# Residual rows turned by VectorE and by loads in runs of 128 bytes instead of TensorE, and filling products dealt 2-4

## The chip, the core and the metric

One core of a Trainium2 chip. The metric is the device time of one execution in microseconds (us); of a kernel several runs are timed and their median is given. TensorE (PE in the profile) multiplies matrices, and also turns tiles by a product with the identity; VectorE (DVE), ScalarE (ACT) and GpSimd (POOL) work elementwise; SyncE (SP) issues almost all DMA transfers, in order, to one queue. DRAM, SBUF (128 partitions) and PSUM (where products land) are the memories.

## What is computed

A trunk of two layers over 1024 tokens of width 1024 in float32: a retention layer, then one projection to keys and values that the second layer shares, then a layer of stick-breaking attention with 8 heads. Both layers end in the same way; the last lines are the ones that matter here.

```python
def reference(x, ..., sb_norm_pre, sb_w_in, sb_w_out, sb_norm_post):
    ...
            u = rms_norm(h, sb_norm_pre[j])
            proj = u @ sb_w_in[j]
            q, g = jnp.split(proj, [SB_QK_WIDTH], axis=-1)
            q = split_heads(q, SB_HEADS).astype(jnp.float32)
            o = stick_breaking_attention(q, k_shared, v_shared)
            o = merge_heads(o).astype(h.dtype) * jax.nn.silu(g)
            y = o @ sb_w_out[j]
            h = h + rms_norm(y, sb_norm_post[j])
    return h
```

`h` on the right of the last line is the residual.

## The kernel before

**Layout.** Tokens are worked in two halves, t=0 (tokens 0 to 511) and t=1 (512 to 1023). In nearly all of the kernel a tile has channels on the partitions and tokens along the row, the turned form; the residual is kept in DRAM in that form, as `h_d[t][u]`, four tensors of 128x1024 per half, each holding two blocks of 128 channels by 512 tokens side by side. A float32 product is made as three products of a high and a low part (`mm3`, lines 413, 414 and 415). `split` (lines 514, 515) makes the two parts: ACT the high one, VectorE the low one.

**The second layer.** Sixteen attention heads-and-halves `n` = 0 to 15 (two heads to an `Att` object, eight objects). For each, `rows` makes scores, VectorE scans them, and `mix` turns the weights on PE (line 1298), multiplies them with the values and calls `gate`, which loads the gate (`sg<-g`), multiplies it with the product in PSUM (line 1326) and splits the result into `oT`. `merge(main, side, ...)` writes one list of steps with others dealt evenly in between. While the first heads run, PE is also fed with the last projection products of the layer before (`P.pieces`, the filler): they end in VectorE's sums of line 888 (`tab<-pma`, `S<-pmb`).

**The end.** The last object's output product is made by `finish(1, heads[7], ys)`. Its steps `prep(0..3)` are dealt into n = 15: they load the output weights (`whl`, `ko`, `A`), the residual (`xh<-h`, one tile of 128x1024 per `u`, four loads of 512 KB in rows of 4 KB) and the gain row (`sgn`). Then `last()` makes, for each of four blocks b of 128 tokens, the output with tokens on the partitions: `piece` (12 products into one bank for 512 channels; VectorE adds what earlier objects gave, ACT sums squares, VectorE scales the sum and multiplies with the gain), `turn(b)` (eight products with the identity that turn the residual of the block from channels to tokens on the partitions, into two PSUM banks, line 1398), and `write(b)` (POOL takes the power −1/2 into `col`, line 1403; VectorE multiplies the row with it and adds the turned residual, line 1406; two stores to the output). The last block's second half is made as two pieces of 256.

**What sets the order.** The program is first written as one list of instructions; then `arrange`, a planner with costs for each operation and due times, sets the order of each engine's queue. So an edit in one place can move rows elsewhere. Tiles come from rings by tag (`xh` 8, `vo` 4, `sg` 4, `AT` 3 buffers and so on), and a tile waits until the readers of the one before it in the ring are done.

Of the kernel before, what the change touches and what calls it, by code (L numbers as in the profile page):

```python
# [13 lines left out]
F32 = mybir.dt.float32  # L14
F32R = mybir.dt.float32r
AF = mybir.ActivationFunctionType
ALU = mybir.AluOpType
# [291 lines left out]
def trunk(ctx, tc, xT, wts, gains, trig, ident_in, cols, last_gain, out):  # L309
# [5 lines left out]
    nc = tc.nc  # L315
# [7 lines left out]
    def S(tag, shape, dt=F32):  # L323
        cnt[0] += 1
        x = sb.tile([128] + list(shape), dt, tag=tag, name=f"{tag}{cnt[0]}", bufs=BUFS[tag])
        tag_of[x[:].tensor.name] = tag
        return x

    def PS(tag):
        cnt[0] += 1  # L330
        x = ps.tile([128, 512], F32, tag=tag, name=f"p{tag}{cnt[0]}", bufs=BUFS[tag])
        tag_of[x[:].tensor.name] = tag
        banks.add(x[:].tensor.name)
        return x
# [24 lines left out]
    def dma(dst, src, eng=nc.sync):  # L359
        return eng.dma_start(dst.bitcast(F32), src.bitcast(F32))  # L360

    keep = tc.keep_in_program_order
    V, A_, G, MM = nc.vector, nc.scalar, nc.gpsimd, nc.tensor.matmul
# [99 lines left out]
    def merge(main, *sides):  # L463


        done = [0] * len(sides)
        for i, m in enumerate(main):
            m()
            for k, (steps, lead, tail) in enumerate(sides):
                n = len(main) - lead - tail  # L470
                upto = min(len(steps), len(steps) * max(0, i + 1 - lead) // n)
                while done[k] < upto:
                    steps[done[k]]()
                    done[k] += 1
# [48 lines left out]

    turned = out[0:512, :].rearrange("a (b t) -> (a b) t", b=2)
    straight = out[512:1024, :]
    st_d = [[dr.tile([128, 512], F32, tag=f"st{h}{d}", name=f"st{h}{d}") for d in range(2)] for h in range(NH)]
    y_d = [[dr.tile([128, 512], F32, tag=f"y{t}{c}", name=f"y{t}{c}") for c in range(8)] for t in range(2)]
    h_d = [[DRAM(f"h{t}{c}", F32) for c in range(4)] for t in range(2)]
# [803 lines left out]
    def c_post(t, y_d, acc):  # L1332
# [22 lines left out]

        return [stat1, stat2, row] + in_turn(8, 1, load, add)

    def finish(t, P, ys):

        w, hs, box = {}, [], {}  # L1360

        def prep(u):
            nh, i = divmod(u, 2)
            x = S("whl", [2, 2, 512], F32R) if u == 0 else None
            for e in range(2):
                r = w[nh, 2 * i + e] = x[:, :, e] if u == 0 else hl("ko" if u == 1 else "A")
                for k in range(2):
                    dma(r[:, :, 256 * k:256 * k + 256],
                        w_d[P.pr][2 * nh + k][i][:].rearrange("p (l e n) -> p l e n", l=2, e=2)[:, :, e])
            a = S("xh", [1024])  # L1370
            dma(a[:], h_d[t][u][:])
            hs.append(a)
            if u == 3:
                box["g"] = S("sgn", [1024])
                dma(box["g"][:], last_gain.broadcast_to([128, D]))

        def piece(b, k, a, n):
            if a == 0:
                box["s"], box["y"] = S("small", [4]), S("AT", [1024])
            p, tl = PS(banks4[box.setdefault("n", 0) % 4]), slice(128 * b, 128 * b + 128)  # L1380
            box["n"] += 1
            nh, cl = a // 512, slice(a % 512, a % 512 + n)
            for e in range(4):
                x, o = w[nh, e], P.oT[e]
                mm3(p[:, :n], o[:, 0, tl], o[:, 1, tl], x[:, 0, cl], x[:, 1, cl], e == 0, e == 3)
            y, q, sm = ys[b][:, nh, cl], S("f2", [512]), box["s"]
            V.tensor_tensor(y, p[:, :n], y, ALU.add)
            A_.activation(q[:, :n], y, AF.Square, accum_out=sm[:, k:k + 1])
            if k == 0:
                V.tensor_scalar(sm[:, 3:4], sm[:, 0:1], 1.0 / D, EPS, ALU.mult, ALU.add)  # L1390
            else:
                V.tensor_scalar(sm[:, 3:4], sm[:, k:k + 1], 1.0 / D, sm[:, 3:4], ALU.mult, ALU.add)
            V.tensor_tensor(box["y"][:, a:a + n], y, box["g"][:, a:a + n], ALU.mult)

        def turn(b):
            box["h", b] = [PS("o" if b % 2 else "z") for _ in range(2)]
            for c in range(8):
                nc.tensor.transpose(box["h", b][c // 4][:, 128 * (c % 4):128 * (c % 4) + 128],
                                    hs[c // 2][:, 512 * (c % 2) + 128 * b:512 * (c % 2) + 128 * b + 128], ident[:])

        def write(b):
            r, y = S("col", [4]), box["y"]
            G.tensor_tensor(r[:, 0:1], box["s"][:, 3:4], mhalf[:, 0:1], ALU.pow)
            for nh in range(2):
                cl = slice(512 * nh, 512 * nh + 512)
                V.scalar_tensor_tensor(y[:, cl], y[:, cl], r[:, 0:1], box["h", b][nh][:], ALU.mult, ALU.add)
                dma(straight[128 * b:128 * b + 128, cl], y[:, cl], nc.scalar if nh else nc.sync)

        def last():
            for b in range(4):  # L1410
                piece(b, 0, 0, 512)
                if b < 3:
                    turn(b)
                for k, a in ((1, 512),) if b < 3 else ((1, 512), (2, 768)):
                    piece(b, k, a, 512 if b < 3 else 256)
                if b == 3:
                    turn(b)
                write(b)

        return [lambda u=u: prep(u) for u in range(4)], last  # L1420
# [131 lines left out]
    def layer_c(units, out, load, kept, post):  # L1552

        kq, gs, vs, _ = units
        order = [(x, n) for x in kq[:3] + [vs[0]] for n in (1, 2)]
        opening = len(order)
        order += [(x, n) for x in [vs[0]] + kq[:3] for n in rest]
        order += [(x, n) for x in kq[3:] + [vs[1]] + gs[:2] for n in full]
        order += [(x, n) for x in gs[2:] for n in (1, 5, 6, 7, 4)]
        fill = len(order)  # L1560
        order += [(x, n) for n in (2, 3) for x in gs[2:]]
        P = Phase(order, (opening, fill))
        first, end, halt = P.marks
        at = P.at
        merge(out[:14], (load, 0, 2))
        P.ensure(1)
        merge(out[14:])

        def scale(kt):
            V.tensor_tensor(kept[kt][:], kept[kt][:], rowh[0][:].unsqueeze(1).broadcast_to([128, 2, 512]), ALU.mult)  # L1570
        post += c_stats(1)
        for j, k in zip((1,2,3,3,4,5,6,7,8,9,10,12,13,14), range(len(post))):
            at[j].append(post[k])
        for j, f in zip((first - 4,first - 3,first - 2,first - 1), w_turn(B.raws, kept, scale)):
            at[j].append(f)
        trays[:] = ["sc0", "sc1", "A"]
        at[first].append(lambda: trays.__setitem__(slice(None), ["sc0", "sc1", "A", "A", "A", "A"]))
        at[first].append(lambda: ring.__setitem__(slice(None), ["wraw", "wraw", "wraw", "vo", "vo"]))
        pres = w_out()
        for k, f in enumerate(pres):  # L1580
            at[first + 30 + (end - first - 30 - 28) * k // len(pres)].append(f)
        heads = [Att(t, p) for t in range(2) for p in range(NPAIR)]

        def rows_of(n):
            return heads[n // 2].rows(n % 2) if n < 16 else []
        r0 = []
        for k in range(4):
            at[end - 4 + k].append(lambda k=k: (r0 or r0.extend(rows_of(0)), r0[k]()))
        for f in P.pieces(0, end):
            f()  # L1590
        filler = P.pieces(end, halt)
        merge(heads[0].mix(0), (filler[:3], 0, 1))
        merge(rows_of(1), (filler[3:6], 0, 0))
        merge(heads[0].mix(1), (filler[6:], 0, 1), (rows_of(2), 0, 1))
        ys, acc = [], []
        for n in range(2, 16):
            A = heads[n // 2]
            if n % 2 == 0:
                L = heads[n // 2 - 1]
                if n % 8 == 2:  # L1600
                    ys = []
                pre, out = L.out(ys, acc if L.t == 0 and L.pr == 3 else None)
                pre[0]()
            extra = []
            if n == 9:
                post = c_post(0, y_d[1], acc)
            if 10 <= n < 14:
                extra = post[3 * n - 30:3 * n - 27]
            if n == 15:
                extra, last = finish(1, heads[7], ys)  # L1610
            merge(A.mix(n % 2), (out[8 * (n % 2):][:8], 0 if n % 2 else 1, 1), (rows_of(n + 1), 0, 1), (extra, 1, 1))
        last()
# [79 lines left out]
```

## Time and profile before

| | us |
|---|---|
| median of 3 runs | 1629.36 |
| the runs | 1628.98 to 1630.21 |
| the profiled execution, its own time | 1628.69 |
| its span (first to last instruction) | 1626.7 |
| PE busy in it | 1619.3 |
| VectorE busy in it | 1219.1 |
| ACT, POOL busy in it | 804.1, 122.1 |

The profile describes the one profiled execution. Its own time is 2.0 us longer than its span, for what lies ahead of the first and behind the last instruction. The median of the timed runs is 0.67 us above the profiled execution. The DMA queues move 386.43 MB in 175890 packets. TensorE's granted clock is full throughout. In rows of the profile, names are the program's tile names without their numbers: `pma`, `pmb`, `pz` and `po` are PSUM banks.

### The profile page before, as it was taken

Reading aid. Unit: us, or ns where it says so; the run is one execution under the profiler, and the core shown is the slowest. Engines: PE = TensorE matmul, PEld = TensorE weight load, DVE = VectorE, ACT = ScalarE, POOL = GpSimd, SP = SyncE. Lnnn points to the kernel's source line nnn. Section 1 sums busy time; section 2 is a strip of 40 time slices with the busy share of each in tenths; the row PEclk is TensorE's granted clock in tenths of the full one; section 3 lists DMA queues with packets and bytes.
Section 4 is the critical chain, followed back from the end, with each engine's and each line's share of the span. In section 5 each row is a group of like instructions: output and inputs, shape, how many; then the busy total and the mean of one; then the engine's idle time right before and its main releaser. Section 6 shows DMA issues by size and latency. Waiting matters only on the chain.

```text
span 1626.7 us, 22505 instructions
## 1 busy us (share of the span) xinstructions
PE 1619.3 (100%) x7659; PEld 1351.5 (83%) x7659; DVE 1219.1 (75%) x1956; ACT 804.1 (49%) x1535; POOL 122.1 (8%) x271
## 2 busy tenths in 40 slices
PE   9999999999999999999999999999999999999998
PEld 7888888888888888888888888888888888888887
DVE  8997866654668888887689877767658666878775
ACT  8553334433456555544356665566544433554432
POOL 0000000000022212211000000000001111010010
PEclk9999999999999999999999999999999999999999
DMA  9556765543377878784776788978337877869781
GB/s 319 188 175 252 247 211 189 208 141 133 112 267 254 308 246 285 234 290 146 242 278 223 260 312 290 344 278 308 119 126 259 314 279 259 282 214 331 253 272 52
DMA packets 175890, 386.43 MB, mean 238 GB/s; under 512 B 18080, under 2 KB 34592, under 8 KB 173216
## 3 DMA queue, kind: packets, MB, share of 16 engines
q1 hardware_dynamic: 175056, 383.93, 68.3%
q8 instruction: 60, 0.98, 0.2%
q10 hardware_dynamic: 720, 1.07, 0.2%
q14 instruction: 54, 0.44, 0.1%
HBM read 263.82 MB, written 121.11 MB: 237 GB/s over the span
## 4 chain that ended last, share of the span: by engine, by line
PE 98%; DMA 1%; DVE 0%; issue 0%; ACT 0%; SPq 0%; DVEq 0%; POOLq 0%; POOL 0%
PE pma L413 12%; PE pma L415 12%; PE pma L414 12%; PE pmb L413 9%; PE pmb L415 9%; PE pmb L414 9%; PE po L414 6%; PE po L415 6%; PE po L413 6%; PE pz L414 3%; PE pz L415 3%; PE pz L413 3%; PE pz L1298 2%; PE pz L770 1%; PE pz L488 0%; DMA wraw<-in_wts_dram 0%
## 5 line engine op out<-in xcount | busy, mean ns | idle before, releaser
L514 ACT ACTIVATE whl<-wraw 128x512 fp32r<-128x512 f32 x266 | 156.2, 625 | 175.1 <-issue 62.6
L515 DVE TENSOR_TENSOR whl<-wraw,whl 128x512 fp32r<-128x512 f32 x266 | 176.1, 686 | 87.0 <-ACT whl L514 84.4
L1270 DVE TENSOR_TENSOR_SCAN sgn<-sgn 128x128 f32<-128x128 f32 (+3 forms) x64 | 86.6, 1352 | 17.3 <-POOL sgn L1268 17.3
L515 DVE TENSOR_TENSOR AT<-pz,AT 128x512 fp32r<-128x512 f32 (+1 forms) x96 | 51.1, 551 | 50.0 <-ACT AT L514 49.6
L514 ACT ACTIVATE AT<-pz 128x512 fp32r<-128x512 f32 (+1 forms) x96 | 45.1, 492 | 68.4 <-PE pz L1298 67.9
L413 PE MATMUL pmb<-oT,whl 128*128 128x512 f32 x192 | 75.9, 395 | 0.0
L415 PE MATMUL pmb<-oT,whl 128*128 128x512 f32 x192 | 75.3, 392 | 0.0
L414 PE MATMUL pmb<-oT,whl 128*128 128x512 f32 x192 | 75.1, 391 | 0.0
L413 PE MATMUL pmb<-qk,whl 128*128 128x512 f32 x184 | 72.5, 394 | 0.0
L415 PE MATMUL pmb<-qk,whl 128*128 128x512 f32 x184 | 72.1, 392 | 0.0
L414 PE MATMUL pmb<-qk,whl 128*128 128x512 f32 x184 | 71.8, 390 | 0.0
L515 DVE TENSOR_TENSOR whl<-vo,whl 128x512 fp32r<-128x512 f32 x62 | 41.7, 689 | 35.1 <-ACT whl L514 34.8
L884 ACT ACTIVATE f<-pma 128x512 f32<-128x512 f32 x52 | 30.7, 595 | 49.7 <-PE pma L415 49.3
L514 ACT ACTIVATE whl<-vo 128x512 fp32r<-128x512 f32 x62 | 37.5, 624 | 34.7 <-PE pma L415 17.5
L413 PE MATMUL pma<-xh,whl 128*128 128x512 f32 x136 | 53.3, 392 | 0.0
L414 PE MATMUL pma<-xh,whl 128*128 128x512 f32 x136 | 53.1, 390 | 0.0
L415 PE MATMUL pma<-xh,whl 128*128 128x512 f32 x136 | 53.1, 390 | 0.0
L1267 POOL TENSOR_SCALAR_AFFINE_SELECT A<-A 128x128 f32<-128x128 f32 x32 | 10.8, 336 | 535.1 <-DMA ko<-k 395.4
L907 ACT ACTIVATE wraw<-wraw,gn 128x256 f32<-128x256 f32 x102 | 45.4, 497 | 7.9 <-DMA wraw<-in_wts_dram 7.9
L1262 ACT ACTIVATE xh<-pz 128x512 f32<-128x512 f32 (+3 forms) x48 | 23.6, 492 | 48.6 <-PE pz L415 48.4
L1263 ACT ACTIVATE sgn<-pz 128x512 f32<-128x512 f32 (+2 forms) x96 | 46.7, 488 | 0.0
L1262 ACT ACTIVATE A<-pz 128x512 f32<-128x512 f32 (+3 forms) x48 | 23.6, 491 | 42.5 <-PE pz L415 42.4
(580 smaller groups left out, 5137.0 us busy)
## 6 DMA issues: line engine op xcount, KB each, us to landing
wraw<-in_wts_dram SPq DMA_DIRECT2D x332, 256.0 KB, 3.8
whl<-w SPq DMA_DIRECT2D x56, 512.0 KB, 6.0
vo<-in_wts_dram SPq DMA_DIRECT2D x70, 256.0 KB, 4.4
xh<-k SPq DMA_DIRECT2D x32, 512.0 KB, 6.8
v<-v SPq DMA_DIRECT2D x32, 512.0 KB, 5.0
k<-A SPq DMA_DIRECT2D x21, 512.0 KB, 4.9
e<-whl SPq DMA_DIRECT2D x10, 1024.0 KB, 6.7
whl<-e SPq DMA_DIRECT2D x10, 1024.0 KB, 6.7
```

Source lines behind the costliest of these rows:

```text
L413: MM(p, lh, rh, start=start, stop=False, **kw)
L414: MM(p, lh, rl, start=False, stop=False, **kw)
L415: MM(p, ll, rh, start=False, stop=stop, **kw)
L514: A_.activation(dst[0], src, AF.Copy)
L515: V.tensor_tensor(dst[1], src, f32(dst[0]), ALU.subtract)
L770: nc.tensor.transpose(pt[:, 128 * e:128 * e + 128], on[:, 128 * e:128 * e + 128], ident[:])
L884: A_.activation(c[:], p[:], AF.Copy)
L907: A_.activation(x, x, AF.Copy, scale=gcol(self.gains[col], 2 * (2 * i + k) + c))
L1262: A_.activation(a[:, o:o + ww], p[:, :ww], AF.Sigmoid)
L1263: A_.activation(n[:, o:o + ww], p[:, :ww], AF.Sigmoid, scale=-1.0)
L1270: V.tensor_tensor_scan(n[:, :W][:, ::-1], n[:, :W][:, ::-1], n[:, :W][:, ::-1], 1.0, ALU.mult, ALU.bypass)
L1298: nc.tensor.transpose(p[:, 128 * tb:128 * tb + 128], self.A[hh][tb][:, c0:c0 + 128], ident[:])
```

## The change

The eight blocks of 128 channels of the second half's residual are turned beforehand, without PE. `turn_h(k)` loads block k, has VectorE transpose it in squares of 32x32 (each square stays where it is), and stores it to a new DRAM tensor `ht_d`. Two of these steps are dealt into each of n = 2 to 5. `prep(u)` then loads the residual of block u with tokens on the partitions: four loads, each taking 32 tokens of 32x32 pieces, 1024 runs of 32 floats (128 bytes). `turn(b)` is gone, and `write(b)` adds `hs[b]` from SBUF. Separately, the six filler steps of the first two merges are dealt two and four instead of three and three.

```diff
+    ht_d = dr.tile([1024, 512], F32, tag="ht", name="ht")
...
+    def turn_h(k):
+        a, x = S("vo", [512]), S("vo", [512])
+        dma(a[:], h_d[1][k // 2][:, 512 * (k % 2):512 * (k % 2) + 512])
+        V.transpose(x[:], a[:])
+        dma(ht_d[128 * k:128 * k + 128, :], x[:])
+
     def finish(t, P, ys):
...
             a = S("xh", [1024])
-            dma(a[:], h_d[t][u][:])
+            for j in range(4):
+                dma(a[32 * j:32 * j + 32, :].rearrange("a (k b) -> a k b", b=32),
+                    ht_d[:].rearrange("(k a) t -> a k t", a=32)[:, :, 128 * u + 32 * j:128 * u + 32 * j + 32])
             hs.append(a)
...
-        def turn(b):
-            box["h", b] = [PS("o" if b % 2 else "z") for _ in range(2)]
-            for c in range(8):
-                nc.tensor.transpose(box["h", b][c // 4][:, 128 * (c % 4):128 * (c % 4) + 128],
-                                    hs[c // 2][:, 512 * (c % 2) + 128 * b:512 * (c % 2) + 128 * b + 128], ident[:])
-
...
-                V.scalar_tensor_tensor(y[:, cl], y[:, cl], r[:, 0:1], box["h", b][nh][:], ALU.mult, ALU.add)
+                V.scalar_tensor_tensor(y[:, cl], y[:, cl], r[:, 0:1], hs[b][:, cl], ALU.mult, ALU.add)
...
-                if b < 3:
-                    turn(b)
...
-                if b == 3:
-                    turn(b)
                 write(b)
...
-        merge(heads[0].mix(0), (filler[:3], 0, 1))
-        merge(rows_of(1), (filler[3:6], 0, 0))
+        merge(heads[0].mix(0), (filler[:2], 0, 1))
+        merge(rows_of(1), (filler[2:6], 0, 0))
...
-            extra = []
+            extra = [lambda k=k: turn_h(k) for k in (2 * n - 4, 2 * n - 3)] if 2 <= n < 6 else []
```

The rows below are lines of the order of one engine's instructions, with the tiles' running numbers, first the kernel before, then the changed one. Line numbers of the changed kernel are higher: 888 becomes 889, 1013 becomes 1014, 1326 becomes 1327, 1387 becomes 1396, 1392 becomes 1401, 1393 becomes 1402, 1406 becomes 1409.

PE among the last products, before (block 0; `pma` is the bank of the products, `pz` the bank of the turned residual, `xh` the residual's tiles):

```order
L413 MATMUL pma2606_15391<-ko2589_15293,qk2560_15160 128x512
L414 MATMUL pma2606_15391<-ko2589_15293,qk2560_15160 128x512
L415 MATMUL pma2606_15391<-ko2589_15293,qk2560_15160 128x512
L1398 MATMUL pz2608_15409<-ident_70,xh2582_15254 128x128 x2
L1398 MATMUL pz2608_15409<-ident_70,xh2590_15296 128x128 x2
L1398 MATMUL pz2609_15410<-ident_70,xh2597_15341 128x128 x2
L1398 MATMUL pz2609_15410<-ident_70,xh2600_15375 128x128 x2
L413 MATMUL pma2610_15419<-A2595_15335,qk2560_15160 128x512
L414 MATMUL pma2610_15419<-A2595_15335,qk2560_15160 128x512
```

The same place in the changed kernel:

```order
L413 MATMUL pma2622_15444<-ko2605_15337,qk2576_15201 128x512
L414 MATMUL pma2622_15444<-ko2605_15337,qk2576_15201 128x512
L415 MATMUL pma2622_15444<-ko2605_15337,qk2576_15201 128x512
L413 MATMUL pma2624_15462<-A2611_15382,qk2576_15201 128x512
L414 MATMUL pma2624_15462<-A2611_15382,qk2576_15201 128x512
L415 MATMUL pma2624_15462<-A2611_15382,qk2576_15201 128x512
```

The products of the second piece follow those of the first at once; the same goes for blocks 1 and 2, and behind the last product nothing is left on PE.

SP while the last head runs, before: weights to `ko` and `whl`, the residual to four `xh` tiles, the gain, and the first store to the output.

```order
L360 DMA ko2589_15293<-w301_229 128x2x256
L360 DMA ko2589_15293<-w311_231 128x2x256
L360 DMA xh2582_15254<-h10_104 128x1024
L360 DMA xh2590_15296<-h11_105 128x1024
L360 DMA whl2581_15249<-w300_228 128x2x256
L360 DMA whl2581_15249<-w310_230 128x2x256
L360 DMA whl2581_15249<-w300_228 128x2x256
L360 DMA whl2581_15249<-w310_230 128x2x256
L360 DMA xh2597_15341<-h12_106 128x1024
L360 DMA xh2600_15375<-h13_107 128x1024
L360 DMA sgn2601_15377<-in_last_gain_dram 128x1024
L360 DMA out_0_dram<-AT2605_15390 128x512
```

The same in the changed kernel, where the four blocks' tiles are `xh2598`, `xh2606`, `xh2613` and `xh2616`:

```order
L360 DMA xh2598_15295<-ht_76 32x32x32
L360 DMA xh2606_15340<-ht_76 32x32x32
L360 DMA whl2597_15290<-w300_229 128x2x256
L360 DMA whl2597_15290<-w310_231 128x2x256
L360 DMA whl2597_15290<-w300_229 128x2x256
L360 DMA whl2597_15290<-w310_231 128x2x256
L360 DMA xh2598_15295<-ht_76 32x32x32
L360 DMA xh2613_15388<-ht_76 32x32x32
L360 DMA xh2616_15425<-ht_76 32x32x32
L360 DMA xh2606_15340<-ht_76 32x32x32
L360 DMA xh2598_15295<-ht_76 32x32x32
L360 DMA ko2605_15337<-w311_232 128x2x256
```

Here seven of the sixteen residual loads and the four of `whl` stand ahead of the second half of `ko`; the other nine residual loads and the gain follow, the last one just ahead of the first store to the output.

VectorE where the first head ends and the second one's scores are scanned, before (a scan prints as SCALAR_TENSOR_TENSOR with line 1270; `sg<-po` are the gate products of the first head, `tab<-pma` the sums of the filler):

```order
L515 TENSOR_TENSOR AT1882_11578<-pz1881_11576,AT1882_11578 128x128
L888 TENSOR_TENSOR tab1831_11275<-pma1885_11623,tab1831_11275 128x512
L1270 SCALAR_TENSOR_TENSOR sgn1894_11658<-sgn1894_11658 128x128
L1013 TENSOR_TENSOR sg1887_11638<-tab1831_11275,sg1887_11638 128x512
L1270 SCALAR_TENSOR_TENSOR sgn1897_11672<-sgn1897_11672 128x256
L1271 TENSOR_TENSOR xh1893_11657<-xh1893_11657,sgn1894_11658 128x127
L1271 TENSOR_TENSOR xh1896_11671<-xh1896_11671,sgn1897_11672 128x255
L888 TENSOR_TENSOR tab1832_11289<-pma1886_11624,tab1832_11289 128x512
L1326 TENSOR_TENSOR sg1889_11643<-po1878_11566,sg1889_11643 128x512
L1270 SCALAR_TENSOR_TENSOR sgn1901_11703<-sgn1901_11703 128x384
L1326 TENSOR_TENSOR sg1890_11648<-po1879_11567,sg1890_11648 128x512
```

The same in the changed kernel:

```order
L515 TENSOR_TENSOR AT1882_11579<-pz1881_11577,AT1882_11579 128x128
L1362 STREAM_TRANSPOSE vo1981_12125<-vo1980_12124 128x512
L1327 TENSOR_TENSOR sg1885_11618<-po1872_11535,sg1885_11618 128x512
L1327 TENSOR_TENSOR sg1886_11623<-po1873_11536,sg1886_11623 128x512
L889 TENSOR_TENSOR tab1831_11276<-pma1893_11653,tab1831_11276 128x512
L1271 SCALAR_TENSOR_TENSOR sgn1890_11633<-sgn1890_11633 128x128
L515 TENSOR_TENSOR oT1884_11617<-sg1885_11618,oT1884_11617 128x512
L1271 SCALAR_TENSOR_TENSOR sgn1897_11673<-sgn1897_11673 128x256
L1272 TENSOR_TENSOR xh1889_11632<-xh1889_11632,sgn1890_11633 128x127
L1272 TENSOR_TENSOR xh1896_11672<-xh1896_11672,sgn1897_11673 128x255
L889 TENSOR_TENSOR tab1832_11290<-pma1894_11654,tab1832_11290 128x512
```

Between the last split of `AT` and the first sum of the filler there now stand the second transpose and both gate products, which were behind the second sum before.

## The prediction

> **What bounds the kernel now.** I read the page first: the busy shares and the chain that ended last.
>
> ```profile
> span 1626.7 us, 22505 instructions
> PE 1619.3 (100%) x7659; PEld 1351.5 (83%) x7659; DVE 1219.1 (75%) x1956; ACT 804.1 (49%) x1535; POOL 122.1 (8%) x271
> ...
> PE 98%; DMA 1%; DVE 0%; issue 0%; ACT 0%; SPq 0%; DVEq 0%; POOLq 0%; POOL 0%
> ```
>
> PE (TensorE) is busy in all but 7 us of the span and carries 98% of the chain. So an instruction taken off PE shortens the run by its own length, as long as PE isn't left waiting; and work added to VectorE (75%) or the DMA queues costs nothing until PE, or the tail behind it, waits for it. Next I asked what PE waits for now (us in total, times, longest):
>
> ```profile
> PE pz L386 <- DVE f L384: 1.7, 1, 1.7
> PE pma L414 <- DVE whl L515: 0.2, 1, 0.2
> PE pma L415 <- DVE xh L515: 0.2, 1, 0.2
> ```
>
> Three waits, 2.1 us, none of them for a DMA; the first belongs to the start of the run. There is almost no wait left to remove, but also no spare time on PE that would swallow a new one.
>
> The third view is the chain at the end of the run (start, length, what):
>
> ```profile
> 1598.60 0.87 PE pz L1398 x8
> ...
> 1604.94 0.87 PE po L1398 x8
> ...
> 1611.30 0.44 PE pz L1398 x4
> ```
>
> L1398 are the turning products of the last stage. Twenty of the 32 stand among the last products and on the chain, 2.18 us together.
>
> **The change, part by part.**
>
> *The 20 turning products on the path.* The timeline of PE around the second group checks the 0.87:
>
> ```profile
> 1604.54 0.40 PE L415 MATMUL pmb<-ko,qk 128*128 128x512 f32 x1
> 1604.77 1.04 PE L1398 MATMUL po<-ident,xh 128*128 128x128 f32 x8
> 1605.57 0.47 PE L413 MATMUL pmb<-A,qk 128*128 128x512 f32 x1
> 1605.88 0.39 PE L414 MATMUL pmb<-A,qk 128*128 128x512 f32 x1
> ```
>
> Products overlap, so I count starts: one product takes 1604.77 − 1604.54 = 0.23. From the first turning product to the second product behind the group are 1.11 us, of which 0.23 would be there anyway: 0.88. The chain says 0.87. Removed: 0.87 + 0.87 + 0.44 = **−2.2 us**, all on the path.
>
> *The last 12 turning products.* They stand behind the last product; here the tail (timeline of all engines):
>
> ```profile
> 1619.82 0.28 PE L415 MATMUL pma<-A,qk 128*128 128x256 f32 x1
> ...
> 1620.14 0.42 DVE L1387 TENSOR_TENSOR sc<-pma,sc 128x256 f32<-128x256 f32 x1 [0.38 <-PE pma L415]
> 1620.38 1.04 PE L1398 MATMUL po<-ident,xh 128*128 128x128 f32 x8
> ...
> 1620.98 0.19 ACT L1388 ACTIVATION_READ_ACCUMULATOR f<-sc 128x1 f32 x1
> 1621.26 0.20 DVE L1392 TENSOR_SCALAR small<-small 128x1 f32<-128x1 f32 x1
> ...
> 1621.38 0.41 DVE L1393 TENSOR_TENSOR AT<-sc,sgn 128x256 f32<-128x256 f32 x1
> 1621.54 0.65 POOL L1403 TENSOR_TENSOR col<-small,mhalf 128x1 f32<-128x1 f32 x1 [4.68 <-DVE small L1392]
> 1622.23 1.41 DVE L1406 SCALAR_TENSOR_TENSOR AT<-AT,col,po 128x512 f32<-128x512 f32 x2 [0.44 <-POOL col L1403]
> ```
>
> They end at 1621.42; the writes that read them start at 1622.23 and wait for `col`, which takes the way product, ACT sum, L1392, POOL. So taking these 12 away brings **0**; what is late there stays late.
>
> *Order in the tail.* Before, the final L1392 starts at 1621.26, though ACT's sum is there at 1621.17, because a write of the third row block stands ahead of it. In the new order two 256-wide gain products (0.41 each, as in the row of L1393) stand there instead. They start when the last sum `sc` is done, 1620.14 + 0.42 = 1620.56, and 1620.56 + 0.82 = 1621.38 is 0.1 after the 1621.26 of now; rows that overlap could make it 0. I take **+0.1**.
>
> *The write from SBUF instead of PSUM.*
>
> ```profile
> L1352 DVE SCALAR_TENSOR_TENSOR wraw<-wraw,gn,acc 128x512 f32<-128x512 f32 x8 | 6.0, 746 | 0.0
> ```
>
> The same operation with all operands in SBUF takes 746 ns; the two in the tail take 1.41 together, pipelined. **0**, with ±0.05 as bounds.
>
> *Eight transposes on VectorE.* No row of before shows that operation. The nearest:
>
> ```profile
> L515 DVE TENSOR_TENSOR whl<-wraw,whl 128x512 fp32r<-128x512 f32 x266 | 176.1, 686 | 87.0 <-ACT whl L514 84.4 <-DMA ga<-f 2.1
> L1270 DVE TENSOR_TENSOR_SCAN sgn<-sgn 128x512 f32<-128x512 f32 x8 | 9.8, 1221 | 4.6 <-POOL sgn L1268 4.6
> 1260.00:1360.00 100.00, 100.00 (x532) 85.99 (x532) 63.49 (x109) 38.52 (x92) 14.69 (x48) 1.00 0.78 275
> ```
>
> An elementwise pass over 128x512 takes 0.69 us, the slowest one of that shape 1.22; I take 0.69, since a transpose within squares makes one pass and carries nothing from element to element. Eight are 5.5 us (at most 9.8). The window (busy us of PE, weight loads, VectorE, ACT, POOL; then PE's clock, the DMA share and GB/s) shows VectorE busy 63.49 of 100 us in the stretch where most of them stand, at full clock. Hidden: **0**. If one stands just ahead of something that PE waits for, it costs up to 0.7; that is in the rival at the first heads.
>
> *The turned copy through DRAM.* Eight loads and eight stores of 256 KB are added, 4.2 MB. At the 354 GB/s of the busiest window (next fence) they are 12 us of DMA in a stretch of some 130 us whose DMA share is 0.78, so there is room for twice that. The loads of keys `xh<-k` that stand behind such a load start up to 0.74 us later (256 KB at 354 GB/s); bounds 0 and 8 × 0.74 = 5.9. I take **0**: no wait of PE for a load is listed, and each added transfer is one of a few dozen.
>
> *Sixteen loads of the residual in runs of 128 bytes, for four in rows of 4 KB.* SP's queue now, the rate while the last loads run, and who needs them:
>
> ```profile
> 1570.35 1.17 SPq L360 DMA_DIRECT2D ko<-w  x2
> 1571.58 1.07 SPq L360 DMA_DIRECT2D xh<-h  x2
> 1572.74 4.13 SPq L360 DMA_DIRECT2D whl<-w  x4
> 1576.97 1.10 SPq L360 DMA_DIRECT2D xh<-h  x2
> ...
> 1576.00:1582.00 6.00, 6.00 (x30) 5.00 (x29) 5.96 (x8) 1.72 (x3) 0.00 (x0) 1.00 1.00 354
> ...
> 1597.74 0.39 PE L413 MATMUL pma<-ko,qk 128*128 128x512 f32 x1
> ...
> L360 SPq DMA_DIRECT2D cc<-in_cols_dram x1: 327/327/327, 11.4 to 11.4; - x1
> ...
> DMA to landing us min/median/max: 4.5/4.5/4.5
> ```
>
> An issue takes SP about 0.55 (1.07 for two), so sixteen are 9 us; SP has nothing else to do until the first store to the output, over 20 us later. The transfers: by bytes a load of 128 KB takes 0.37 us at 354 GB/s, all sixteen 5.9: as much as the four old ones. By runs: `whl` moves in runs of 1 KB, 256 of them in 256 KB, which is 0.74 us or 2.9 ns a run; a residual load has 1024 runs, so 2.96 us, and sixteen 47 us. These are my two ends. When does it hurt? Transfers start at 1571.6. Beside the residual, 5.2 us of weights and gains (1.8 MB) go through the same engines, and a landing costs some 2 us more. The last residual block is read at 1622.23 − 2.2 = 1620.0. So 16384 runs may take 1620.0 − 2.0 − 1571.6 − 5.2 = 41.2 us: 2.5 ns a run. Up to there it is **0**; above, 16 us for each ns more. The second half of `ko`, now behind seven residual loads and the four of `whl`, comes to the same limit: at 2.9 ns it lands near 1571.6 + 20.7 + 3.7 + 2.0 = 1598.0, needed at 1597.74. I take the near end: the DMA engines were fully busy with bytes in that window, so 2.9 ns there is the price of 1 KB and not of a run, and the only load in runs of 128 bytes (`cc`, 128 of them) landed in 4.5 us, no later than others.
>
> The Trainium skill, "DMA: Bandwidth & Descriptors", section "Specifications", speaks against the change: transfers under 512 B don't reach line rate, since the engine then reads, modifies and writes. No row of before has enough of them to show it; what it would do here is worked out with the second rival. The page's section "Bandwidth" measures a floor of about 10.5 ns per packet on an engine; an estimate from it is 64 × 10.5 ns = 0.67 us a load and 10.8 us for sixteen, which is in time.
>
> *Filling products dealt 2-4, and what moves with them.* The rows of the first heads:
>
> ```profile
> 1236.41 0.32 SPq L360 DMA_DIRECT2D g<-sg  x1
> ...
> 1240.52 0.93 SPq L360 DMA_DIRECT2D sg<-g  x2
> ...
> 1243.85 0.69 DVE L888 TENSOR_TENSOR tab<-pma,tab 128x512 f32<-128x512 f32 x1 [2.31 <-PE pma L415]
> 1245.05 0.51 DVE L1270 TENSOR_TENSOR_SCAN sgn<-sgn 128x128 f32<-128x128 f32 x1 [0.51 <-POOL sgn L1268]
> 1245.75 0.69 DVE L1013 TENSOR_TENSOR sg<-tab,sg 128x512 f32<-128x512 f32 x1 [0.20 <-ACT sg L1012]
> ...
> DMA to landing us min/median/max: 2.0/4.7/6.2
> ```
>
> The same products are made, so the dealing itself costs 0. But on VectorE one transpose and the two gate products now stand ahead of the sum `tab<-pma`, where VectorE was idle for 2.31 us; the gate products wait for the two loads `sg<-g`. If these are late, all that follows on VectorE is late: the sum, the scans, and the weights that PE turns for the next product. The loads now follow the store that was issued at 1236.41 with one other load between, so they go out between 1237 and 1240.5; I take 1239.2. With the median landing of 4.7 they are there at 1243.9, and two gates of 0.68 end at 1245.3: 1.4 late. VectorE takes back the gaps of 0.51 and 0.20 shown, and later does not have the gates to do. So 0 to +0.7 on PE here; I take **0**, and the slow end is the first rival.
>
> *Sum.* −2.2 + 0 + 0.1 + 0 = −2.1. The profiled execution took 1628.69 (span 1626.7 and 2.0 around it), so 1626.6; the median of the runs, 1629.36, lies 0.67 above it: **1627.3**. That is 0.13% less. About 0.2% (3.3 us) is what a measurement of this kernel can tell from no change: faster begins below 1626.1, slower above 1632.6.
>
> **The rivals.**
>
> *A wait at the gate loads.* With the longest landing, 6.2, the loads are there at 1245.4, the gates end at 1246.8, 2.9 after the time at which the sum ran before; less the 0.7 of gaps, PE stalls about 2 us. For it: VectorE takes its rows in order, and PE has no reserve. Against: the order is made so that loads come in time, and 4.7 is the usual landing. Time: 1627.3 + 2.0 = 1629.3; the gain is given back.
>
> *Late residual loads (slower).* At 2.9 ns a run the last one is there at 1571.6 + 47.4 + 5.2 + 2.0 = 1626.2, for a need at 1620.0: +6.2, so 1633.5. It decides from 2.5 ns a run on. The same price has a second mechanism: if a run of 128 bytes takes the engines as long as 512, read and written again, that is 8 times its bytes, 8 × 5.9 = 47 us. With four times (no second pass) it is 24 us, and nothing is late. For it: the high end above, and runs an eighth as long as the shortest in that window. Against: no row says that a run costs as much as 1 KB. The Trainium skill's rule on transfers under 512 B (the same page and section) is the second mechanism.
>
> **How the numbers follow.** The forecast (all hidden, turning products gone) 0.68, with a range of its own of 1626.0 to 1628.4, since the three runs of before spread over 1.2 us (1628.98 to 1630.21) and the moved rows may cost or bring a few tenths; some 0.08 of it lies below 1626.1. The wait at the gates 0.2: 1628.4 to 1630.5. The late loads 0.1: above 1632.6 nearly all. The remaining 0.02 are waits elsewhere. So faster 0.08, same 0.82, slower 0.10, and the range from 1625.8 to 1631.0 leaves out the late loads and a little at the low end.
>
> **What would show it.** No row of `ident,xh` in the last 30 us of PE, and products there 0.23 apart throughout: the −2.2. The final POOL `col` about 2.1 earlier, and VectorE's last writes waiting for it and not for `xh`: the 0 of the 12 and of the loads. Transposes near 0.69 on VectorE with PE at 100% between 1230 and 1400. It is wrong if the waits of PE list `ko` or VectorE's `whl` or `xh`, if a write waits for a DMA `xh<-ht`, or if a gate product waits for `sg<-g` and the sum behind it for the gate.

## The result, and the profile after

| | before | changed |
|---|---|---|
| median of 22 runs, us | 1630.38 | 1627.81 |
| lowest to highest | 1628.98 to 1631.91 | 1626.60 to 1629.33 |
| profiled execution, its own time | 1628.69 | 1627.50 |
| its span | 1626.7 | 1625.5 |

The changed kernel is 2.6 us faster by the medians; the ratio is 0.9985, with a 95% interval of 0.9979 to 0.9991. The interval leaves out 1, so there is a gain, but it lies within the 0.2% that I set as "no change"; the predicted 1627.3 is 0.5 below the median. The ratios here and below are estimated from all the runs, with an interval, so they aren't quite the quotients of the medians beside them. The page of the changed kernel, the lines that answer to those of before:

```profile
span 1625.5 us, 22487 instructions
PE 1616.3 (99%) x7627; PEld 1348.2 (83%) x7627; DVE 1223.8 (75%) x1964; ACT 804.2 (49%) x1535; POOL 125.4 (8%) x271
...
DMA packets 194258, 390.62 MB, mean 240 GB/s; under 512 B 34912, under 2 KB 51424, under 8 KB 191584
...
PE 98%; DVE 1%; ACT 1%; DMA 1%; issue 0%; SPq 0%; DVEq 0%; POOLq 0%; POOL 0%
```

PE has 32 products less, VectorE eight instructions more, and the packets under 512 bytes rose from 18080 to 34912: the 16384 runs of 128 bytes are there. PE's waits in the changed kernel:

```profile
PE pz L386 <- DVE f L384: 1.7, 1, 1.7
PE pma L413 <- ACT sg L885: 0.5, 1, 0.5
PE pma L414 <- DVE whl L515: 0.3, 1, 0.3
PE pma L415 <- DVE xh L515: 0.2, 1, 0.2
```

The columns are, as in the prediction, us in total, times, longest. There is none for a load, none for a transpose, none for a gate product. The wait of 0.5 is at 17.5 us, long before anything that the change touched.

**A profile's start differs from one execution to the next.** The spans differ by only 1.2, less than the medians do. PE's rows come in the same order in both kernels up to some 1243 us, so a product in that part can serve as a mark. Here is the same one, in the profile of before:

```profile
1230.19 0.39 PE L415 MATMUL pz<-xh,xh 128*128 128x512 f32 x1
```

and in that of the changed kernel:

```profile
1231.42 0.39 PE L415 MATMUL pz<-xh,xh 128*128 128x512 f32 x1
```

The changed kernel was 1.23 late there, by nothing that was changed: 0.9 of it arose in the first 50 us. From the mark to the end of the span it is 396.5 before and 394.1 after: **−2.4 us**, which fits the medians. I use this distance for all experiments.

Where the 2.4 went shows at the end of the run. The last stage begins with this product, before:

```profile
1595.70 0.39 PE L413 MATMUL pma<-whl,qk 128*128 128x512 f32 x1
```

and in the changed kernel with this one; the further rows stand where the first group of turning products stood:

```profile
1596.98 0.39 PE L413 MATMUL pma<-whl,qk 128*128 128x512 f32 x1
...
1599.24 0.39 PE L414 MATMUL pma<-ko,qk 128*128 128x512 f32 x1
1599.47 0.39 PE L415 MATMUL pma<-ko,qk 128*128 128x512 f32 x1
1599.70 0.39 PE L413 MATMUL pma<-A,qk 128*128 128x512 f32 x1
```

From the mark to the first product of the stage it is 365.51 before and 365.56 after, so nothing was won or lost on the way there.

The 512-wide products of the stage now follow each other at 0.23 without a break. And the tail, all engines:

```profile
1618.77 0.28 PE L415 MATMUL pma<-A,qk 128*128 128x256 f32 x1
...
1620.21 0.21 DVE L1401 TENSOR_SCALAR small<-small 128x1 f32<-128x1 f32 x1
1620.50 0.55 POOL L1406 TENSOR_TENSOR col<-small,mhalf 128x1 f32<-128x1 f32 x1 [4.69 <-DVE small L1401]
1621.08 1.41 DVE L1409 SCALAR_TENSOR_TENSOR AT<-AT,col,xh 128x512 f32<-128x512 f32 x2 [0.66 <-POOL col L1406]
```

The last product starts 387.35 after the mark, against 389.63 before: −2.28 on PE, all of it in the last stage. From there to the final writes it is 2.31, against 2.41: another −0.10, in POOL's step (0.55 instead of 0.65). The writes still wait for `col` alone.

### The profile page after: what moved, and what is told of

Read it like the earlier page. It is cut to its first block, busy times and chain, and to the rows that moved or that the text cites. A ratio compares the mean times of both kernels' runs of the same rounds, so it can differ in the third digit from the quotient of the medians.

```text
span 1625.5 us, 22487 instructions
## 1 busy us (share of the span) xinstructions
PE 1616.3 (99%) x7627; PEld 1348.2 (83%) x7627; DVE 1223.8 (75%) x1964; ACT 804.2 (49%) x1535; POOL 125.4 (8%) x271
## 2 busy tenths in 40 slices
DMA packets 194258, 390.62 MB, mean 240 GB/s; under 512 B 34912, under 2 KB 51424, under 8 KB 191584
## 4 chain that ended last, share of the span: by engine, by line
PE 98%; DVE 1%; ACT 1%; DMA 1%; issue 0%; SPq 0%; DVEq 0%; POOLq 0%; POOL 0%
PE pma L413 12%; PE pma L415 12%; PE pma L414 12%; PE pmb L413 9%; PE pmb L415 9%; PE pmb L414 9%; PE po L414 6%; PE po L415 6%; PE po L413 6%; PE pz L415 3%; PE pz L414 3%; PE pz L413 3%; PE pz L1299 2%; PE pz L771 1%; PE pz L488 0%
## 5 line engine op out<-in xcount | busy, mean ns | idle before, releaser
L1264 ACT ACTIVATE sgn<-pz 128x512 f32<-128x512 f32 (+2 forms) x96 | 46.7, 488 | 0.0
L678 POOL TENSOR_SCALAR_AFFINE_SELECT sc<-sc 128x256 fp32r<-128x256 f32 x16 | 11.7, 748 | 444.3 <-DMA v<-va 408.7
```

What stands on the lines that cost most here:

```text
L1264: A_.activation(n[:, o:o + ww], p[:, :ww], AF.Sigmoid, scale=-1.0)
```

## The experiments

Ten runs. The table gives each with its distance from the mark to the span's end in its one profile, and the median of its timed runs against the runs of before on the same chip. Those medians are of ten or eleven runs, for runs_of_32_bytes and transposes_times_8 of four. A distance is read to a tenth; the timed runs alone settle a difference only to about 1.5 us.

| run | mark to end, us | median | before beside it | ratio (95%) |
|---|---|---|---|---|
| before | 396.5 | | | |
| changed | 394.1 | 1627.81 | 1630.38 | 0.9985 (0.9979 to 0.9991) |
| turns_on_path | 396.5 | 1629.96 | 1630.04 | 1.0003 (0.9994 to 1.0012) |
| turns_at_end | 394.0 | 1628.48 | 1630.04 | 0.9990 (0.9981 to 0.9998) |
| deal24_only | 398.1 | 1632.06 | 1630.04 | 1.0010 (1.0002 to 1.0019) |
| deal33_else_changed | 396.4 | 1630.07 | 1630.04 | 1.0002 (0.9993 to 1.0011) |
| gate_first | 398.5 | 1631.12 | 1629.98 | 1.0003 (0.9994 to 1.0012) |
| deal33_copies | 396.5 | 1629.97 | 1629.98 | 0.9999 (0.9990 to 1.0008) |
| transposes_priced | 394.0 | 1627.51 | 1629.98 | 0.9982 (0.9972 to 0.9991) |
| runs_of_32_bytes | 404.1 | 1637.97 | 1629.98 | 1.0043 (1.0029 to 1.0056) |
| transposes_times_8 | 402.3 | 1636.89 | 1629.58 | 1.0047 (1.0030 to 1.0064) |
| runs_of_4_bytes | 989 | 2222.26 (one run) | 1629.58 | |

The first four ask which part of the change brought the gain.

### turns_on_path

```diff
+        def turn(b):
+            z = box["h", b] = [PS("o" if b % 2 else "z") for _ in range(2)]
+            for c in range(8):
+                nc.tensor.transpose(z[c // 4][:, 128 * (c % 4):128 * (c % 4) + 128],
+                                    hs[c // 2][:, 512 * (c % 2) + 128 * b:512 * (c % 2) + 128 * b + 128], ident[:])
...
-                V.scalar_tensor_tensor(y[:, cl], y[:, cl], r[:, 0:1], hs[b][:, cl], ALU.mult, ALU.add)
+                V.scalar_tensor_tensor(y[:, cl], y[:, cl], r[:, 0:1], box["h", b][nh][:], ALU.mult, ALU.add)
```

> The changed kernel with the 32 turning products put back where they were: each write waits for them and adds their banks instead of the loaded tile (they turn a tile that is turned already, so the output is not the residual's sum). Loads, VectorE's transposes and the dealing 2-4 stay. Theory A (the gain is the 20 turning products that left PE's path, all else costs nothing): 2.2 to 2.4 us slower than the changed kernel, so equal to the kernel before within 0.4 us. Rival B (the dealing or the moved rows brought the gain): stays about 2 us under the kernel before.

396.5, the distance of before to a tenth, and the time of before. So the loads in short runs, the detour through DRAM, VectorE's transposes and the new dealing cost nothing together; the whole gain hangs on the turning products. POOL's last step takes 0.65 again, as before.

### turns_at_end

The same `turn(b)`, at the same places in the program, with the write reading `hs[b]` again.

> The changed kernel with the 32 turning products still made, but nothing reads their banks, so the planner puts all of them behind the last product. Theory A: PE ends some 3.6 us later (32 x 0.11), at about 1622.4 of a span of 1625.5, still ahead of the last store's landing, so the time is that of the changed kernel, 2.5 us under the kernel before. Rival C (turning products cost their length wherever they stand): 3.6 us slower than the changed kernel, so 1 us over the kernel before.

PE in its tail:

```profile
1617.87 0.28 PE L415 MATMUL pma<-A,qk 128*128 128x256 f32 x1
1617.99 1.04 PE L1407 MATMUL pz<-ident,xh 128*128 128x128 f32 x8
...
1620.62 1.04 PE L1407 MATMUL po<-ident,xh 128*128 128x128 f32 x8
```

All 32 are made, behind the last product, and end at 1621.66 of a span of 1624.6. The distance is that of the changed kernel; the timed runs are faster than before (0.9990) and agree with it, though they alone wouldn't tell 1 us of cost from none. Theory A holds in both directions: what counts is not the number of turning products but whether one stands ahead of a product of the chain.

### deal24_only and deal33_else_changed

```diff
-        merge(heads[0].mix(0), (filler[:3], 0, 1))
-        merge(rows_of(1), (filler[3:6], 0, 0))
+        merge(heads[0].mix(0), (filler[:2], 0, 1))
+        merge(rows_of(1), (filler[2:6], 0, 0))
```

This edit put into the kernel before, and taken out of the changed one.

> The kernel before with only the filler dealt 2-4. Theory A: the same as the kernel before within 0.4 us. Rival B: 2 us faster.

> The changed kernel with the filler dealt 3-3 as before. Theory A: 2.2 to 2.5 us faster than the kernel before, like the changed kernel. Rival B: no faster than the kernel before. If the dealing is there to make room for the first transposes, 0.5 to 1 us of the gain is lost.

Neither theory gave this. The dealing 2-4 makes the kernel before 1.6 us slower, and leaving it out of the changed kernel loses its whole gain (396.4). PE's waits with the dealing alone:

```profile
PE pz L386 <- DVE f L384: 1.7, 1, 1.7
PE po L413 <- DVE sg L1326: 1.3, 1, 1.3
PE pma L413 <- ACT sg L884: 0.6, 1, 0.6
```

and VectorE and PE at that place:

```profile
1278.88 0.56 DVE L1271 TENSOR_TENSOR xh<-xh,sgn 128x383 f32<-128x383 f32 x1
1280.13 1.23 DVE L1270 TENSOR_TENSOR_SCAN sgn<-sgn 128x512 f32<-128x512 f32 x1 [0.69 <-POOL sgn L1268]
1281.27 0.67 DVE L1326 TENSOR_TENSOR sg<-po,sg 128x512 f32<-128x512 f32 x1
...
1280.19 0.48 PE L415 MATMUL pmb<-oT,whl 128*128 128x512 f32 x1
1281.99 0.50 PE L413 MATMUL po<-AT,v 128*128 128x512 f32 x1 [1.33 <-DVE sg L1326]
```

The next `po` product needs the bank that the gate product reads, and the gate product stands behind a scan, which waits for POOL. From start to start PE loses 1.80 − 0.23 = 1.57, the whole difference. With 3-3 and the rest of the change, the loss lies nearby, between 1274 and 1283, in five smaller waits:

```profile
PE pz L413 <- ACT sgn L1264: 0.5, 2, 0.3
PE pz L1299 <- DVE xh L1272: 0.4, 1, 0.4
...
PE po L413 <- DVE sg L1327: 0.3, 1, 0.3
PE pz L1299 <- DVE AT L515: 0.2, 1, 0.2
```

They are 1.4 together; counted from start to start, as above, the five cost 0.48, 0.37, 0.42, 0.59 and 0.49, which is 2.35 and again the whole difference.

### gate_first

In the planner, behind `order = best[1]`, the two rows of VectorE above are exchanged; all other queues stay word for word.

```diff
+    line = order['DVE']; i = next(i for i, k in enumerate(line) if steps[k].outs[0].tensor.name.startswith('sg1940') and any(b.tensor.name.startswith('po1923') for b in steps[k].ins))
+    line[i - 1], line[i] = line[i], line[i - 1]
```

> The kernel before with the filler dealt 2-4, and two neighbouring rows of VectorE's queue exchanged by hand: the gate product that PE waits for (1.6 us at 1280 in the run with the dealing alone) goes ahead of the 512-wide scan that stood in front of it. Nothing else moves on any queue. Theory D (the dealing by itself costs nothing; what cost 1.5 to 2 us was this one row, which stood behind a scan that waited for GpSimd while PE waited for its bank): the wait of PE for the gate goes from 1.3 to under 0.3, and the time is 1.3 to 1.6 us lower, within 0.5 us of the kernel before. Rival E (the gate's load is late, so the gate can't go earlier): the wait stays, and the time stays 1.5 to 2 us over the kernel before.

```profile
1281.34 0.69 DVE L1326 TENSOR_TENSOR sg<-po,sg 128x512 f32<-128x512 f32 x1 [1.01 <-DMA sg<-g]
1281.95 1.21 DVE L1270 TENSOR_TENSOR_SCAN sgn<-sgn 128x512 f32<-128x512 f32 x1
...
1282.09 0.50 PE L413 MATMUL po<-AT,v 128*128 128x512 f32 x1 [0.52 <-DVE sg L1326]
```

Neither theory fits alone. PE's wait for the gate fell from 1.33 to 0.52, but not to nothing, since the gate product now stood there for its load, for 1.01. And the scan, now behind the gate product, began late and held up the split of `oT` that follows it, for which PE then waited at 1284.6:

```profile
PE pma L414 <- DVE oT L515: 0.6, 1, 0.6
```

So the exchange moved the loss by a row and didn't remove it: the distance is 398.5, against 398.1 without it (this profiled execution was the slowest of its eleven). The median is 0.9 lower than that of the dealing alone, each taken against before, but the two intervals overlap, so a gain isn't shown. How much of the 1.6 is the row's place and how much the late gate load, these runs don't settle.

### deal33_copies

```diff
-        V.transpose(x[:], a[:])
+        V.tensor_copy(x[:], a[:])
```

> The changed kernel with the filler dealt 3-3, and VectorE's eight transposes replaced by copies of the same tiles (so the residual that is added is not turned within its squares). All queues have the same rows in the same order as in the run with 3-3; a copy is what the planner's cost supposes (0.36 us of VectorE), a transpose took 0.61 to 0.70. Theory F (the order that the planner found at 3-3 is what loses the 2.2 us): the same as that run, 2.2 us over the changed kernel, with PE's waits at 1273 to 1283 unchanged. Rival G (the transposes' time on VectorE, under-priced by the planner, pushes later rows late): 1.5 to 2.5 us faster than that run, PE's waits there gone.

396.5, the median that of before, and among PE's waits the same four lines as above, word for word, though a copy takes VectorE 0.42 where a transpose takes 0.70. The order loses the time, not the length of the transposes. Adding `turn_h` makes the planner arrange the first heads anew; what it finds at 3-3 has these waits, what it finds at 2-4 has none.

### transposes_priced

```diff
-        if s.op == "InstTensorTensor":
+        if s.op == "InstTensorTensor" or "ranspose" in s.op:
```

> The changed kernel (2-4) with one line of the planner's costs changed: a transpose on VectorE is priced like a TENSOR_TENSOR of its size (0.64 us busy) instead of like a copy. The order moves in 60 to 130 lines on PE, VectorE and SP. If the low price cost anything in the changed kernel, up to 0.8 us is to be had (the waits of PE listed there beyond the start: 0.5, 0.3 and 0.2). Theory A: within 0.5 us of the changed kernel. Theory F (any move of the order can cost 1 to 2.5 us at the first heads): from the same up to 2.5 us slower, with a wait of PE between 1240 and 1310 to show it.

The same as the changed kernel: 394.0, and a median 0.3 lower, which is within the scatter. The order moved again, and this time there is no wait of PE past 1230. It beats the kernel before (0.9982, 0.9972 to 0.9991), the changed kernel not measurably.

### transposes_times_8

```diff
-        V.transpose(x[:], a[:])
+        for _ in range(8):
+            V.transpose(x[:], a[:])
```

> The changed kernel with each of VectorE's eight transposes made eight times over (same output): 56 more, 0.61 us of VectorE each, 34 us between 1230 and 1380, where it is idle some 36% of the time, 54 us. The planner orders them anew, under-priced as before. Theory A (VectorE's spare time hides them): at most 3 us slower than the changed kernel, and that by waits of the kind seen at 3-3. Rival J (VectorE's transposes reach PE's path in proportion, so that the eight cost something that the removed products hide): 10 us or more slower.

Busy time between 1230 and 1380 us in the changed kernel, and then in this one (PE, weight loads, VectorE, ACT, POOL):

```profile
1230.00:1380.00 150.00, 150.00 (x786) 128.29 (x786) 106.93 (x174) 62.44 (x143) 22.69 (x66) 1.00 0.88 310
```

```profile
1230.00:1380.00 150.00, 145.98 (x754) 122.41 (x753) 132.81 (x225) 57.91 (x133) 21.09 (x63) 1.00 0.83 289
```

and the longest waits of PE in this one that the changed kernel doesn't have:

```profile
PE pz L1299 <- DVE xh L1272: 1.2, 1, 1.2
PE po L414 <- DVE AT L515: 1.1, 2, 0.7
PE pma L414 <- DVE qk L515: 0.9, 1, 0.9
```

8.2 us slower for 56 more (402.3 against 394.1; 9.1 by the medians, which are of four runs here): about 0.15 each, not the 0.61 that each takes, but far more than the 3 us that theory A allowed and close to the 10 of rival J. VectorE is then 89% busy, and its rows reach PE late. Rival J's reason, a cost in proportion that the eight would have too, isn't borne out: 8 × 0.15 would be 1.2 us, and turns_on_path, which has the eight and the turning products, is at the distance of before to a tenth. Between the eight that cost nothing and the 64 the cover runs out; where, was not tried.

### runs_of_32_bytes and runs_of_4_bytes

```diff
+                for c in range(4):
+                    o = 8 * c
-                dma(a[32 * j:32 * j + 32, :].rearrange("a (k b) -> a k b", b=32),
-                    ht_d[:].rearrange("(k a) t -> a k t", a=32)[:, :, 128 * u + 32 * j:128 * u + 32 * j + 32])
+                    dma(a[32 * j:32 * j + 32, :].rearrange("a (k b) -> a k b", b=32)[:, :, o:o + 8],
+                        ht_d[:].rearrange("(k a) t -> a k t", a=32)[:, :, 128 * u + 32 * j + o:128 * u + 32 * j + o + 8])
```

and, for the other, a load by the access pattern alone:

```diff
+            for c in range(8):
+                dma(a[:, 128 * c:128 * c + 128],
+                    h_d[t][c // 2][:, 512 * (c % 2) + 128 * u:512 * (c % 2) + 128 * u + 128].rearrange("p t -> t p"))
```

> The changed kernel with each residual load cut into four loads of 8 floats a run: 64 loads, 65536 runs of 32 bytes, the same bytes. In the changed kernel sixteen loads landed 0.64 us apart, 0.63 ns a run. Theory H (a run costs about 0.6 ns and an issue on SP 0.56 us, so the loads have a margin of four): 64 loads take 36 to 42 us from 1573, the last lands at 1613 to 1619, before it is read at 1620: the same time, at most 1.5 us slower. Rival I (a run costs 2.5 ns or more, as from the rate at 1 KB): 164 us or more, so over 100 us slower.

> VectorE's transposes stay but are not used: each residual tile is loaded straight from the tensor with channels on the rows, transposed by the access pattern of eight loads per tile, 32 loads, 524288 runs of 4 bytes for the same 2 MB. Theory H (the engines charge by the run, 0.63 to 0.71 ns each from the runs of 128 and 32 bytes): 330 to 370 us from 1573, so the last one lands near 1920 and the time is near 1930 us. Rival K (below some size a run costs more, read and written again in DRAM or SBUF): 2000 us or more. Rival L (by bytes): 1628 to 1640.

The residual's loads in the changed kernel, from the view of the tensor `ht`:

```profile
L360 SPq DMA_DIRECT2D xh<-ht x16: 430/642/3546, 1572.2 to 1592.0; - x16
...
DMA to landing us min/median/max: 2.9/3.7/5.8
```

SP's rows with runs of 32 bytes, and the write that waited for the loads:

```profile
1583.18 42.28 SPq L360 DMA_DIRECT2D xh<-ht  x58
...
1625.55 4.07 DVE L1411 SCALAR_TENSOR_TENSOR AT<-AT,col,xh 128x512 f32<-128x512 f32 x6 [4.57 <-DMA xh<-ht]
```

and SP's row with runs of 4 bytes:

```profile
1696.58 495.17 SPq L360 DMA_DIRECT2D xh<-h  x26
```

In 32 bytes a load of 1024 runs takes 42.28 / 58 = 0.73 us, 0.71 ns a run; in 4 bytes, with 16384 runs, 495.17 / 26 = 19.0 us, 1.16 ns a run. In 128 bytes the last of the sixteen was issued at 1592.0 and landed 3.3 later, at 1595.3; with the 5.2 us for the other 1.8 MB and 2 for the landing that leaves at most 1595.3 − 1572.2 − 7.2 = 15.9 us for 16384 runs, 0.97 ns. So in this range a load costs by the run, at 0.7 to 1.2 ns, and not by the byte.

Not all of that is the DMA engines' own time. Here are the queue's packets and its share of the 16 engines' time, in runs of 32 bytes (1590 to 1624 us) and then of 4 bytes (1600 to 2100 us):

```profile
q1 hardware_dynamic: 49806, 1.57, 81.3%
```

```profile
q1 hardware_dynamic: 412701, 3.22, 45.5%
```

A packet took 34000 × 16 × 0.813 / 49806 = 8.9 ns of an engine in the first and 500000 × 16 × 0.455 / 412701 = 8.8 ns in the second: the same, for an eighth of the bytes. With 4 bytes the engines stood idle more than half of the time, while SP was held by each issue for about as long as a load took. What sets the pace there isn't settled.

Theory H has its kind of cost right for 32 bytes and its time wrong: 10.1 us slower (404.1 against 394.1), where it allowed 1.5. It left out the 5.2 us of weights and gain in the same queue, and 64 loads at 0.73 are 47 us and not 36 to 42, so the last was issued near 1625. It also asked only when the last block is read: the first write already waited for its tile until 1625.55, which means that the pieces of a tile are spread over nearly the whole row of loads, and six writes queued up behind it. For 4 bytes H held in neither number: the run is 1.6 times dearer than in 32 bytes, and the time, 2222, lies where rival K put it. K's reason, bytes read and written again, isn't shown: the packets took the engines no longer.

## Why the prediction was right, by its steps

**The 20 turning products, −2.2.** Right. PE gained 2.28 in the last stage, and putting them back costs 2.4 with POOL's 0.10 (turns_on_path).

**The last 12, 0.** Right: even all 32 cost nothing there (turns_at_end).

**Order in the tail, +0.1.** Wrong in sign, by 0.2 in all. The last small sum starts 1.44 after the last product in both kernels. What I did not see is that the gain product that no longer follows it had run beside POOL's step and lengthened that by 0.10.

**The write from SBUF, 0.** Right: 1.41 for the last two in both.

**Eight transposes, 0.69 each and hidden.** Right in price and in place:

```profile
L1362 DVE STREAM_TRANSPOSE vo<-vo 128x512 f32<-128x512 f32 x8 | 5.6, 702 | 0.0
```

**The copy through DRAM, 0, and the loads in short runs, 0.** Right. No row on PE or VectorE waits for `ht`. The near end that I took, by bytes, is 5.9 / 16384 = 0.36 ns a run, and the far end 2.9. The price lies between them, at most 0.97; that is under the limit of 2.5 that I worked out, so the rival of late loads did not occur. The limit itself was too generous, as the runs of 32 bytes show: it allowed 41.2 us for the loads, they took 64 × 0.73 = 46.7, and the time rose by 10.1 and not by 5.5, because other writes than the last one waited too. The estimate from the Trainium skill's price of a packet ("DMA: Bandwidth & Descriptors", section "Bandwidth"; I read it as on one engine), 0.67 us a load of 1024 packets, is near the 0.73 measured in runs of 32 bytes; for 16384 runs of 4 bytes it would give 10.8 us, and the trace shows 19.0, with the engines 45.5% busy. Its warning on transfers under 512 B (section "Specifications") is true of bytes per second, 174 GB/s at a DMA share of 0.96 between 1585 and 1594 us, against 354 before, and did not matter here:

```profile
1585.00:1594.00 9.00, 9.00 (x52) 7.67 (x51) 3.23 (x6) 2.35 (x5) 0.00 (x0) 1.00 0.96 174
```

**The dealing, 0.** The sum was right, the step was not, and that it came out at 0 is luck. I wrote that the same products are made, so the dealing itself costs nothing, and looked at one place, the gate loads at 1243. There I was right (the view of the tile `sg`, and VectorE's timeline, both of the changed kernel):

```profile
L360 SPq DMA_DIRECT2D sg<-g x2: 320/320/320, 1239.4 to 1240.0; - x2
...
DMA to landing us min/median/max: 3.1/3.7/4.3
```

```profile
1244.22 1.29 DVE L1327 TENSOR_TENSOR sg<-po,sg 128x512 f32<-128x512 f32 x2 [0.83 <-PE po L415]
```

The loads went out at 1239.4, 0.2 later than estimated, landed in at most 4.3, and the gates waited for PE and not for them. But an edit of the order is paid wherever the planner then moves something: the dealing alone costs 1.6 at 1282, the rest of the change alone (3-3) 2.4 at 1274 to 1283, and only both together nothing. I saw neither loss, so I couldn't have known that neither arises when both parts are made. A relative of my first rival is what the dealing alone shows, 40 us further on: a gate product late on VectorE, there behind a scan and not behind its load, while PE waits.

**The base.** I summed against the profiled execution of before and its 3 runs. Of the twelve profiles at hand that execution reached the mark earliest: the others were 0.4 to 2.2 later, and the median of 22 runs of before is 1.0 above that of the 3. So my base was 1.0 too low; and the gain was forecast at 2.1 and measured at 2.6, 0.5 too small. The two errors have opposite signs, and the absolute time came out only 0.5 too low: here too there was some luck.

## What to carry to other kernels

An instruction taken off the engine that bounds the run is worth its length only if a product of the chain stands behind it; the same 32 turning products cost 2.4 us with 20 of them among the last products, and nothing with all of them behind the last one. A transpose of float32 can leave TensorE by way of squares of 32 on VectorE and loads in runs of 128 bytes, as long as the loads are issued well ahead (here the last one had landed at 1595.3, and the first write was at 1605.0) and VectorE has slack (here it was 71% busy). Where a planner sets the order, take an edit apart on the chip before believing that a part of it is free: two parts that each cost 1.6 to 2.4 us can cost nothing together, and the place of the loss is not the place of the edit.

## What the runs showed of the hardware

The step of POOL on 128x1 takes 0.54 to 0.56 us alone and 0.65 where a VectorE instruction with two SBUF operands runs on beside it for 0.25: so in all four profiles in which that instruction stood there (before, turns_on_path, deal24_only, gate_first), and 0.54 to 0.55 in the other eight, in which nothing ran beside it. Two other instructions of POOL, in the profile of before, show the same more plainly. They are alike in length when alone (0.29):

```profile
1573.18 0.66 DVE L1235 TENSOR_TENSOR sc<-pmb,sc 128x512 f32<-128x512 f32 x1
1573.31 0.29 POOL L1267 TENSOR_SCALAR_AFFINE_SELECT xh<-xh 128x128 f32<-128x128 f32 x1 [2.48 <-ACT xh L1262]
1573.76 1.08 DVE L1271 TENSOR_TENSOR xh<-xh,sgn 128x895 f32<-128x895 f32 x1
1573.85 1.14 POOL L1268 TENSOR_SCALAR_AFFINE_SELECT sgn<-sgn 128x128 f32<-128x128 f32 x1 [0.24 <-DVE sc L1235]
```

Beside a VectorE instruction that reads a PSUM bank (`pmb`) POOL's takes its 0.29; beside one with both operands in SBUF that still has 0.99 to run it takes 1.14, which is 0.85 more. The delay is what was left of VectorE's instruction, less 0.14; at the tail that gives 0.25 − 0.14 = 0.11, as seen. The Trainium skill ("SBUF — State Buffer", section "SBUF: two separate sides") says that the two share a pair of ports as an exclusive lock, on VectorE's side for two SBUF inputs; the trace agrees: POOL gets no further until VectorE's instruction is done.

The twelve profiled executions have the same rows on PE up to the mark. They drift apart there by up to 1.7 us in their first 50 us and by up to 1.2 between 450 and 500 us, and by less than 0.1 elsewhere: up to the mark, nearly all of the scatter from run to run comes from those two places.
